# Shared first weight tiles, 512-column values and a wide first norm in a two-layer hybrid decoder

## The chip, the core and the metric

The kernel runs on one core of one Trainium2 chip. A core has engines that each work through their own list of instructions in order: TensorE (PE, matrix products), VectorE (DVE), ScalarE (ACT), GpSimd (POOL) and SyncE (SP, which here only starts transfers). They meet at semaphores. The metric is the time of one execution on the device in microseconds (us), lower is better.

## What is computed

The input is x, 512 positions of 1024 channels in float32. Each of two layers does this:

```python
h = rmsnorm(x, norm1_w[l])
proj = h @ w_in[l]
lx, lg, rq, rk, rv, rg, hq, hf, hi, hg = jnp.split(proj, split_idx, axis=-1)
y_lru = rglru_group(lx, lg, ...)                  # 512 channels
y_ret = retention_group(rq, rk, rv, rg, ...)      # 4 heads of 64
y_hg = hgrn2_group(hq, hf, hi, hg, lb_all[l], ...)  # 4 heads of 64
x = x + jnp.concatenate([y_lru, y_ret, y_hg], axis=-1) @ w_out[l]
h = rmsnorm(x, norm2_w[l])
x = x + conv_ffn(h, ffn_w_up[l], ..., ffn_w_down[l])
```

and a last rmsnorm follows. `rmsnorm` divides by the root of the mean square over the channels and multiplies by a weight. In the HGRN2 group the forget gate is f = lb + (1 − lb)·sigmoid(hf), the key is (1 − lb)·sigmoid(−hf), and the values are the columns `hi`, called hv below; the retention group has queries rq, keys rk and values rv. In both groups a state gathers key times value, so a factor of each position can sit on either. The outputs of both groups are normed by head and gated by rg and hg.

## The kernel before

**Tiles.** x lies as eight tiles x0 to x7 of 128 channels by 512 positions. Full float32 accuracy is had from three products in a rounded format: each operand is split in a high part (xh, wh, written by ACT) and the rest (xl, wl, written by DVE), and `mm3` (line 320) issues high·high, high·rest and rest·high, lines 321 to 323. A product of one weight tile (1024 channels by 128 columns, as 128x1024) is 8 times 3 matmuls into one PSUM bank of 128x512, `pps`. The norm's division by position is left out of the operands and multiplied in when DVE copies the bank out (`ev`, with `rb`, which holds 1/root for every position in 128 equal rows).

**What sets the order.** A planner (`Flow`, `Timed`) runs when the kernel is built: the work is written as chains (generators) that are advanced by estimated costs of operations, and the order in which they ask is the fixed order of every engine's list. `next_w` keeps two weight tiles split ahead of the one in use; transfers go through SP. Waits on banks go through `Slots`: four banks for the products (`mm`), four for small ones (`sm`).

**The first norm** (`finish_norm`, line 419). The squares of x0 to x7 are added into `ssq` (in layer 0 by DVE, in layer 1 by POOL). Four fp32 matmuls give the mean square of each position as a column (`rms_ps`, 128x4), DVE makes the root's reciprocal in 12 tiny operations (`rsqrt_cols`), four more matmuls spread it over the rows (`rms_rps`), ACT copies that to `rb`. The columns (`rms_rc`) also scale the values when ACT copies them out. The second norm of a layer goes another way (`rsqrt_wide`, line 358): two matmuls of 512 columns against ones, then Ln, Exp and Square on ACT and two DVE operations.

**Order of the input products.** hf0 hq0 hf1 hq1 (the f and q of HGRN2, two tiles of 128 columns each), hv, rq0 rk0 rv rq1 rk1, lx0 to lx3, hg0 hg1 rg0 rg1 lg0 to lg3, then the output product `ops`. Tiles go in pairs; in layer 0 the first pair is run part by part as its weights land. `hv` and `rv` are each computed with positions on the rows, in 256 columns: `vps`, 2 layers by 192 matmuls. While the last input products run, DVE has what follows the mixers to do: the norms of the head outputs (`hc_v` to `hc_x`), their gating (`rt_on`, `hg_on`), the recurrence of the RG-LRU (`qp`, `lr_g`), and the split of the results (`xl<-hg_on` first) on which `ops` waits.

**Small set-ups.** `setup_lb` (line 480) makes lb and 1 − lb (`sm_m`, `sm_e`, `lbc`), `setup_small` (line 449) the constants of the RG-LRU (`sp_*`, `lamc`).

Of the kernel before, what the change touches and what calls it, by code (L numbers as in the profile page):

```python
# [15 lines left out]
S = 512  # L16
# [12 lines left out]


FIRST = ["x0", 0, "x1", 1, "x2", "x3", 2, "x4", "x5", 3, "x6", "x7"]
# [17 lines left out]
for _n, _w in (  # L49
# [9 lines left out]
WCOL = {"lx": 0, "lg": 512, "hg": 2816, "rg": 1792}  # L59
TAIL = "lx0 lx1 lx2 lx3 hg0 hg1 rg0 rg1 lg0 lg1 lg2 lg3".split()  # L60
TAIL = [(t[:2], int(t[2])) for t in TAIL]

WIN = (
    [("f", 2304), ("f", 2048), ("f", 2432), ("f", 2176), ("v", 2560, 0), ("v", 2560, 1)]
    + [("f", 1024), ("f", 1280), ("v", 1536, 0), ("v", 1536, 1), ("f", 1152), ("f", 1408)]
    + [("f", WCOL[n] + 128 * j) for n, j in TAIL]
)
WNAMES = (
    [("hf", 0), ("hq", 0), ("hf", 1), ("hq", 1), "hv", None]
    + [("rq", 0), ("rk", 0), "rv", None, ("rq", 1), ("rk", 1)]  # L70
    + TAIL
)
# [136 lines left out]
def kernel(ctx, tc, x_in, win, wout, wup, wdn, lruw, params, consts, out):  # L209
# [26 lines left out]
    lbc = const.tile([128, DEPTH, 2, 2], F32, name="lbc")  # L236
# [25 lines left out]
    for l in range(DEPTH):  # L262
        wlist += [win[l, i] for i in range(len(WIN))]
# [94 lines left out]
    def rsqrt_wide(sq, r, tile_of, weights, name):  # L358
# [11 lines left out]
        A.activation(out=r, in_=ps, func=AF.Ln, bias=eps)  # L370
        yield None
        A.activation(out=r, in_=r, func=AF.Exp, scale=-0.5)
        yield None
        t = sq
        A.activation(out=t, in_=r, func=AF.Square)
        yield None
# [8 lines left out]
    def new_norm(nw, pool):  # L385
        n = Norm()
        n.pool = pool
        n.nw, n.h, n.lo, n.sq, n.rb = nw, {}, {}, 0, None
        n.ssq = None
        n.fast = n.wide = False  # L390
        return n
# [27 lines left out]
    def finish_norm(n):  # L419
        if n.wide:  # L420

            v = rpool.tile([128, S], F32, name="rb")
            yield from rsqrt_wide(n.ssq, v, lambda t, i: rpool.tile([128, S], t, name="sq", bufs=3), ones, "rms_ps")
            n.rb = v
            return
# [3 lines left out]
        yield None  # L429
        rc = rsqrt_cols(rpool, ps, [128, NC], "rms")  # L430
        drop(sm)
        yield None
        n.rc = rc
        ps = yield from psum([128, S], "rms_rps")
        for c in range(NC):
            small(0.22, out=ps[:, c * 128:(c + 1) * 128], lhsT=rc[:, c:c + 1].to_broadcast([128, 128]), rhs=ident)
        yield None
        rb = rpool.tile([128, S], F32, name="rb")
        A.activation(out=rb, in_=ps, func=AF.Copy)
        drop(sm)  # L440
        yield None
        n.rb = rb
# [6 lines left out]
    def setup_small():  # L449
        tp = rpool  # L450
        for l in range(DEPTH):
            lam = pc(l, "lam", 0, 4)
            ab = tp.tile([128, 4], F32, name="sp_ab")
            V.tensor_scalar(out=ab, in0=lam, scalar1=-1.0, scalar2=None, op0=ALU.mult)
            rl = tp.tile([128, 4], F32, name="sp_rl")
            V.tensor_scalar(out=rl, in0=ab, scalar1=0.0, scalar2=None, op0=ALU.max)
            V.tensor_tensor(out=ab, in0=ab, in1=lam, op=ALU.max)
            e = tp.tile([128, 4], F32, name="sp_e")
            A.activation(out=e, in_=ab, func=AF.Exp, scale=-1.0)
            yield None  # L460
            z = tp.tile([128, 4], F32, name="sp_z")
            V.tensor_scalar(out=z, in0=e, scalar1=2.0, scalar2=None, op0=ALU.add)
            V.reciprocal(out=z, in_=z)
            V.tensor_tensor(out=z, in0=z, in1=e, op=ALU.mult)
            z2 = tp.tile([128, 4], F32, name="sp_z2")
            V.tensor_tensor(out=z2, in0=z, in1=z, op=ALU.mult)
            yield None
            s = tp.tile([128, 4], F32, name="sp_s")
            V.tensor_scalar(out=s, in0=z2, scalar1=1.0 / 17.0, scalar2=1.0 / 15.0, op0=ALU.mult, op1=ALU.add)
            for d in (13, 11, 9, 7, 5, 3, 1):  # L470
                V.tensor_tensor(out=s, in0=s, in1=z2, op=ALU.mult)
                V.tensor_scalar(out=s, in0=s, scalar1=1.0 / d, scalar2=None, op0=ALU.add)
                yield None
            V.tensor_tensor(out=s, in0=s, in1=z, op=ALU.mult)
            V.scalar_tensor_tensor(out=s, in0=s, scalar=2.0, in1=rl, op0=ALU.mult, op1=ALU.add)
            for i, f in enumerate((-8.0, -16.0, 8.0)):
                V.tensor_scalar(out=lamc[:, l, :, i], in0=s, scalar1=f, scalar2=None, op0=ALU.mult)
            yield None

    def setup_lb():  # L480
# [18 lines left out]
    def matmul_tiles(n, count, done, first=False, freed=None, joint=False):  # L499


        i = 0
        while i < count:
# [7 lines left out]
            if pair == 1:  # L511
                order = [(0, k) for k in range(KD)]
            else:
                cut = KD - 2
                order = [(p, k) for ks in (range(cut), range(cut, KD)) for p in range(2) for k in ks]
                if joint:
                    order = [(p, k) for k in range(KD) for p in range(2)]
            for p, k in order:
                (wh, wl), ps = got[p]
                if k not in n.lo:  # L520
                    yield lambda: k in n.lo
                o = k * 128
                if joint and pair == 2:
                    wh, wl = got[k // 4][0]
                    o = k % 4 // 2 * 512 + p * 256 + k % 2 * 128
                sl = slice(o, o + 128)
                mm3(ps, wh[:, sl], wl[:, sl], n.h[k], n.lo[k], k == 0, k == KD - 1)
                if freed and i == count - 1:
                    freed(k)
                yield None  # L530
                if k == KD - 1:
                    done(i + p, ps)
# [3 lines left out]
    def mixers(l, n):  # L536
# [8 lines left out]

        def evac(key):
            yield lambda: key in ps_of and n.rb is not None
            yield from ev.take()
            t = mp.tile([128, S], F32, name="ev", bufs=NEV)
            V.tensor_tensor(out=t, in0=ps_of.pop(key), in1=n.rb, op=ALU.mult)  # L550
# [4 lines left out]
        def evac_v(key):  # L555
            yield lambda: key in ps_of and n.rb is not None
# [946 lines left out]
```

## Time and profile before

| | |
|---|---|
| median of 3 runs | 1168.36 us (1167.86 to 1168.49) |
| the profiled execution | 1168.12 us |
| its span, first to last instruction | 1166.3 us |
| granted TensorE clock, mean | 0.998 |
| PE busy | 1154.9 us, 99% |
| DVE busy | 781.1 us, 67% |
| ACT busy | 534.3 us, 46% |
| POOL busy | 64.9 us, 6% |
| chain of work that ended last | PE 96%, DVE 2%, DMA 1% |

The span is the time from the first to the last recorded instruction, 1.82 us short of the execution. Busy time of PE counts overlapping matmuls by their modelled ends; how fast PE really issues is read from the starts of matmuls in the timeline. The chain is followed back from the last instruction to what released each step.

### The profile page before, as it was taken

To read this page: it belongs to the slowest core of one execution; us is meant where nothing else is said; L and a number is where in the kernel's file an instruction comes from. 1 tells how busy PE (TensorE), PEld (TensorE's weight loads), DVE (VectorE), ACT (ScalarE), POOL (GpSimd) and SP (SyncE) were. 2 spreads that over 40 slices of the span, in tenths; PEclk is the share of its full clock that TensorE was granted. 3 is DMA by queue.
4 is the path that set the end of the run, shared out by engine and by line. 5 is a ranking of instruction groups with operands and counts; after the bars stand their busy time and mean duration, and the time that the engine had idled before them with its cause. 6 is when DMAs were issued, how large, how long until landed. Compare 5 with 4: busy or idle time off the path is not lost.

```text
span 1166.3 us, 15226 instructions
## 1 busy us (share of the span) xinstructions
PE 1154.9 (99%) x6046; PEld 961.6 (82%) x6046; DVE 781.1 (67%) x1162; ACT 534.3 (46%) x722; POOL 64.9 (6%) x51
## 2 busy tenths in 40 slices
PE   9999999999999999999999999999999999999997
PEld 7888778888888888888888877888888888888886
DVE  7887887577774575474668486955876646745645
ACT  6536874464443343232542568545444424433422
POOL 1011210000000000000310012100000000000001
PEclk9999999999999999999999999999999999999999
DMA  7232223223323332322432221423232232233222
GB/s 257 94 99 56 72 73 125 92 90 106 93 76 105 109 87 89 113 86 76 126 103 81 73 82 37 140 88 98 91 99 96 80 121 93 76 105 104 82 71 88
DMA packets 36455, 111.79 MB, mean 96 GB/s; under 512 B 4512, under 2 KB 5024, under 8 KB 36384
## 3 DMA queue, kind: packets, MB, share of 16 engines
q1 hardware_dynamic: 34560, 108.59, 29.6%
q10 hardware_dynamic: 1824, 2.23, 0.7%
q8 instruction: 47, 0.77, 0.3%
q14 instruction: 24, 0.20, 0.0%
HBM read 106.61 MB, written 2.10 MB: 93 GB/s over the span
## 4 chain that ended last, share of the span: by engine, by line
PE 96%; DVE 2%; DMA 1%; issue 0%; SPq 0%; ACT 0%; POOLq 0%; POOL 0%; DVEq 0%
PE pps L321 20%; PE pps L323 19%; PE pps L322 19%; PE dps L322 7%; PE dps L321 7%; PE dps L323 7%; PE ops L322 3%; PE ops L321 2%; PE ops L323 2%; PE vps L321 1%; PE vps L322 1%; PE vps L323 1%; PE k_o L327 1%; PE hg_pl L327 1%; PE lr_ps L327 1%; DVE qp L185 1%
## 5 line engine op out<-in xcount | busy, mean ns | idle before, releaser
L321 PE MATMUL pps<-xh,wh 128*128 128x512 f32 x1024 | 403.5, 394 | 0.0
L323 PE MATMUL pps<-xh,wl 128*128 128x512 f32 x1024 | 399.4, 390 | 1.3 <-DVE wl L185 1.3
L322 PE MATMUL pps<-xl,wh 128*128 128x512 f32 x1024 | 398.9, 390 | 0.0
L185 ACT ACTIVATE wh<-raw 128x1024 fp32r<-128x1024 f32 (+3 forms) x211 | 204.8, 973 | 150.5 <-PE dps L322 103.3
L185 DVE TENSOR_TENSOR wl<-raw,wh 128x1024 fp32r<-128x1024 f32 (+3 forms) x211 | 243.2, 1155 | 12.8 <-ACT wh L185 12.8
L321 PEld LDWEIGHTS pps<-xh,wh 128*128 128x128 f32 x1024 | 192.5, 188 | 43.2 <-issue 3.5
L323 PEld LDWEIGHTS pps<-xh,wl 128*128 128x128 f32 x1024 | 192.3, 188 | 42.5 <-DVE wl L185 2.1
L322 PEld LDWEIGHTS pps<-xl,wh 128*128 128x128 f32 x1024 | 192.6, 188 | 39.0 <-DVE xl L185 0.4
L185 DVE SCALAR_TENSOR_TENSOR hs<-pps,rb 128x512 f32<-128x512 f32 x88 | 60.4, 690 | 129.6 <-PE pps L323 129.6
L321 PE MATMUL dps<-gh,wh 128*128 128x512 f32 x320 | 124.5, 389 | 0.0
L322 PE MATMUL dps<-gl,wh 128*128 128x512 f32 x320 | 124.5, 389 | 0.0
L323 PE MATMUL dps<-gh,wl 128*128 128x512 f32 x320 | 124.5, 389 | 0.0
L185 DVE TENSOR_TENSOR x<-x,dps 128x512 f32<-128x512 f32 (+1 forms) x72 | 44.9, 627 | 107.4 <-PE dps L323 107.0
L185 ACT ACTIVATE cg<-hs,prm 128x512 f32<-128x512 f32 x44 | 35.9, 816 | 85.1 <-DVE hs L185 85.1
L185 ACT ACTIVATE cg<-cg 128x512 f32<-128x512 f32 x44 | 27.8, 632 | 93.9 <-DVE cg L185 93.9
L321 PEld LDWEIGHTS dps<-gh,wh 128*128 128x128 f32 x320 | 60.1, 188 | 12.6
L323 PEld LDWEIGHTS dps<-gh,wl 128*128 128x128 f32 x320 | 60.1, 188 | 12.4
L322 PEld LDWEIGHTS dps<-gl,wh 128*128 128x128 f32 x320 | 60.1, 188 | 12.4
L185 DVE SCALAR_TENSOR_TENSOR cvv<-hs,prm,cvv 128x511 f32<-128x511 f32 x88 | 65.9, 748 | 1.8
L185 DVE SCALAR_TENSOR_TENSOR cg<-hs,prm,cg 128x511 f32<-128x511 f32 x88 | 65.7, 747 | 1.5
L185 ACT ACTIVATE gh<-cvv 128x512 fp32r<-128x512 f32 x44 | 27.8, 631 | 73.6 <-DVE cvv L185 73.6
L322 PE MATMUL ops<-xl,wh 128*128 128x512 f32 x128 | 50.1, 391 | 0.0
(218 smaller groups left out, 1275.1 us busy)
## 6 DMA issues: line engine op xcount, KB each, us to landing
raw<-in_wup_dram SPq DMA_DIRECT2D x88, 512.0 KB, 3.5
raw<-in_win_dram SPq DMA_DIRECT2D x46, 512.0 KB, 3.5
raw<-in_wdn_dram SPq DMA_DIRECT2D x48, 384.0 KB, 3.0
raw<-in_wout_dram SPq DMA_DIRECT2D x16, 512.0 KB, 3.5
raw<-in_wdn_dram SPq DMA_DIRECT2D x16, 256.0 KB, 2.6
x<-in_x_dram SPq DMA_DIRECT2D x8, 256.0 KB, 5.3
sw<-ev ACTq DMA_DIRECT2D x32, 64.0 KB, 2.1
raw<-in_win_dram SPq DMA_DIRECT2D x4, 256.0 KB, 5.0
```

Of the source, the lines that this page charges most:

```text
L185: return fn(*args, **kw)
L321: T.matmul(out=ps, lhsT=ah, rhs=bh, start=start, stop=False)
L322: T.matmul(out=ps, lhsT=ah, rhs=bl, start=False, stop=False)
L323: T.matmul(out=ps, lhsT=al, rhs=bh, start=False, stop=stop)
L327: T.matmul(**kw)
```

## The change

**The first four tiles.** hf0, hf1, hq0 and hq1 become one block of 512 columns, stored by parts: a weight tile q holds channels tiles k = 2q and 2q + 1 of all four. `joint_tiles` runs them in both layers, all four products for k = 0 to 5 and then k = 6, 7 of each. In layer 0 x and the parts are loaded in turn, x0, part 0, x1, part 1 and so on.

**Values.** hv and rv, 512 columns together, follow at once: one bank for each 128 positions, matmuls of 512 columns. Two of the four banks are small ones (`sm`). ACT copies them out without a scale.

**First norm.** It is made by `rsqrt_wide` in both layers, with a root on ACT and a reciprocal of 128x512 on DVE in place of Ln and Exp. In layer 1 the squares are added by DVE too (`n.fast`). Its scale, no longer on the values, goes on the keys: on k of HGRN2 in the DVE operation that scales it anyhow, and on rk by evacuating it with rb squared, which ACT makes once per layer.

**Set-ups.** `setup_lb` now stands before the end of the first norm; `setup_small` does both layers at once, mostly on POOL. The ones are made by memset.

```diff
-FIRST = ["x0", 0, "x1", 1, "x2", "x3", 2, "x4", "x5", 3, "x6", "x7"]
+JOINT = [("hf", 0), ("hf", 1), ("hq", 0), ("hq", 1)]
+ALONE = "rq0 rk0 rq1 rk1 lx0 lx1 lx2 lx3 hg0 hg1 rg0 rg1 lg0 lg1 lg2 lg3".split()
...
 def rsqrt_wide(...)
+        if root:
+            A.activation(out=t, in_=ps, func=AF.Sqrt, bias=eps)
+            yield None
+            V.reciprocal(out=r, in_=t)
+            V.tensor_tensor(out=t, in0=r, in1=r, op=ALU.mult)
...
 def finish_norm(n):
-        ps = yield from psum([128, NC], "rms_ps")
-        for c in range(NC):
-            small(0.21, out=ps[:, c:c + 1], lhsT=n.ssq[:, c * 128:(c + 1) * 128], rhs=dmean)
...
-        rc = rsqrt_cols(rpool, ps, [128, NC], "rms")
...
-            small(0.22, out=ps[:, c * 128:(c + 1) * 128], lhsT=rc[:, c:c + 1].to_broadcast([128, 128]), rhs=ident)
...
+        yield from rsqrt_wide(n.ssq, v, lambda t, i: rpool.tile([128, S], t, name="sq", bufs=3), ones, "rms_ps", n.root)
...
+    def joint_tiles(n, done):
+        ws, pss = [], []
+        order = [(k, p) for k in range(KD - 2) for p in range(4)] + [(k, p) for p in range(4) for k in (KD - 2, KD - 1)]
+        for k, p in order:
...
+            mm3(pss[p], wh[:, o:o + 128], wl[:, o:o + 128], n.h[k], n.lo[k], k == 0, k == KD - 1)
...
 def evac(key):
-            V.tensor_tensor(out=t, in0=ps_of.pop(key), in1=n.rb, op=ALU.mult)
+                A.activation(out=rb2[0], in_=n.rb, func=AF.Square, scale=0.5)
...
+            if key[0] == "rk":
+                V.tensor_tensor(out=t, in0=ps_of.pop(key), in1=rb2[0], op=ALU.mult)
+            else:
+                V.scalar_tensor_tensor(out=t, in0=ps_of.pop(key), scalar=-0.5, in1=n.rb, op0=ALU.mult, op1=ALU.mult)
...
 def hg_forget(ft):
-            V.tensor_scalar(out=kt, in0=kt, scalar1=olb, scalar2=None, op0=ALU.mult)
+            V.scalar_tensor_tensor(out=kt, in0=kt, scalar=lbc[:, l, ft, 2:3], in1=n.rb, op0=ALU.mult, op1=ALU.mult)
...
 def mixers(l, n):
-                        for k in range(4):
-                            sl = slice(k * 256, (k + 1) * 256)
...
+                for k in (2 * q, 2 * q + 1):
+                    sl = slice(k % 2 * 512, k % 2 * 512 + 512)
+                    mm3(banks[c], n.h[k][:, ts], n.lo[k][:, ts], wh[:, sl], wl[:, sl], k == 0, k == KD - 1)
...
 def main():
+            tile_w(6)
+            tile_w(7)
+            fetch()
+            setup_lb()
```

How DVE's list changes at two places follows; the names are those of the tiles above, and "x7" behind a row is a count.

The first place is DVE around the first norm of layer 0. Before, from the last split of the start to the norm's tiny operations:

```order
L185 TENSOR_TENSOR wl<-raw,wh 128x1024
L185 TENSOR_TENSOR ssq<-ssq,sq 128x512 x7
L185 TENSOR_TENSOR wl<-raw,wh 128x1024 x2
L185 TENSOR_SCALAR rms_v<-rms_ps 128x4
L185 TENSOR_SCALAR rms_rc<-rms_v 128x4
```

After, a piece that begins within the set-up of lb, whose first row (`sm_m<-prm`) follows right on the seventh addition to `ssq` and on the two halves of the split of part 6 and 7:

```order
L175 TENSOR_TENSOR lbc<-sm_e 128x2
L175 TENSOR_SCALAR lbc<-lbc 128x2 x2
L175 TENSOR_TENSOR wl<-raw,wh 128x1024
L175 TENSOR_TENSOR sq<-ssq,sq 128x512
L175 TENSOR_TENSOR wl<-raw,wh 128x1024
L175 RECIPROCAL rb<-ssq 128x512
L175 TENSOR_TENSOR ssq<-rb 128x512
L175 SCALAR_TENSOR_TENSOR ssq<-rms_ps,ssq 128x512
L175 SCALAR_TENSOR_TENSOR rb<-ssq,rb 128x512
L175 SCALAR_TENSOR_TENSOR ev<-pps,rb 128x512 x4
```

The set-up of lb, 14 tiny operations now, and a weight split stand between the additions and `sq<-ssq,sq`, which is the rest of the split sum: the second of the norm's two matmuls reads it. Before, that set-up stood behind the norm's operations.

The second place is DVE in layer 0 while the last gate products run. The copies out of the two rg tiles stand a few rows above each piece, with the four `qp<-qp,lr_g` operations behind them. Before, from the last of the four:

```order
L185 SCALAR_TENSOR_TENSOR qp<-qp,lr_g_1504 128x512
L185 TENSOR_TENSOR wl<-raw,wh 128x1024 x2
L185 TENSOR_TENSOR ev<-pps,rb 128x512
L185 SCALAR_TENSOR_TENSOR rt_on<-rt_on,prm,ev 128x512 x2
L185 TENSOR_TENSOR qp<-qp,lr_g_1288 128x512
```

After, from the end of the second head norm of retention:

```order
L175 SCALAR_TENSOR_TENSOR hc_nt<-hc_nt,hc_v 128x8
L175 SCALAR_TENSOR_TENSOR hc_x<-hc_nt,hc_rc 128x512
L175 SCALAR_TENSOR_TENSOR ev<-pps,rb 128x512
L175 TENSOR_TENSOR wl<-raw,wh 128x1024
L175 SCALAR_TENSOR_TENSOR rt_on<-rt_on,prm,ev 128x512
L175 TENSOR_TENSOR rt_on<-rt_on,hn_rps 128x512
L175 SCALAR_TENSOR_TENSOR rt_on<-rt_on,prm,ev 128x512
L175 TENSOR_TENSOR qp<-qp,lr_g_1121 128x512
```

That head norm (`hc_v` to `hc_x`, 12 operations) and the operation that applies it (`rt_on<-rt_on,hn_rps`) stood ahead of the copies out of rg before, and stand behind them and behind the four `qp` rows now.

## Rows read from the trace of the kernel before

**Rows 1.** Waits of PE: engine, line, releaser, us in total, times, longest.

```profile
PE pps L323 <- DVE wl L185: 1.3, 2, 0.6
```

**Rows 2.** Timeline, PE, values: start us, us, operation, shapes, count, [idle before].

```profile
38.06 0.28 PE L322 MATMUL vps<-wl,xh 128*128 128x256 f32 x1
...
39.98 0.28 PE L323 MATMUL vps<-wh,xl 128*128 128x256 f32 x1
```

**Rows 3.** Timeline, PE, from the start to behind layer 0's first norm.

```profile
5.25 0.79 PE L321 MATMUL pps<-xh,wh 128*128 128x512 f32 x1
...
7.15 0.39 PE L322 MATMUL pps<-xl,wh 128*128 128x512 f32 x1
...
20.37 0.39 PE L323 MATMUL pps<-xh,wl 128*128 128x512 f32 x1
21.33 1.05 PE L327 MATMUL rms_ps<-csm,ssq 128*128 128x1 f32 x8 [0.57 <-DVE ssq L185]
22.25 0.48 PE L321 MATMUL pps<-xh,wh 128*128 128x512 f32 x1
...
25.52 0.39 PE L323 MATMUL pps<-xh,wl 128*128 128x512 f32 x1
25.86 1.16 PE L327 MATMUL rms_rps<-csm,rms_rc 128*128 128x128 f32 x8
26.77 0.48 PE L321 MATMUL pps<-xh,wh 128*128 128x512 f32 x1
```

**Rows 4.** Timeline, PE, first norm of layer 1, first of its two blocks.

```profile
590.03 0.95 PE L327 MATMUL rms_ps<-csm,ssq 128*128 128x1 f32 x8
590.84 0.48 PE L321 MATMUL pps<-xh,wh 128*128 128x512 f32 x1
```

**Rows 5.** Timeline, PE, second norm of layer 0, by wide products.

```profile
231.86 0.63 PE L327 MATMUL rms_ps<-sq,ones 128*128 128x512 f32 x2
232.32 0.39 PE L321 MATMUL pps<-xh,wh 128*128 128x512 f32 x1
```

**Rows 6.** Timeline, DVE, start and first norm of layer 0.

```profile
4.93 0.75 DVE L185 SCALAR_TENSOR_TENSOR xl<-x,prm,xh 128x512 fp32r<-128x512 f32 x1 [3.91 <-ACT xh L185]
...
10.48 1.41 DVE L185 SCALAR_TENSOR_TENSOR xl<-x,prm,xh 128x512 fp32r<-128x512 f32 x2
11.81 0.68 DVE L185 TENSOR_TENSOR wl<-raw,wh 128x512 fp32r<-128x512 f32 x1
...
15.81 5.47 DVE L185 TENSOR_TENSOR ssq<-ssq,sq 128x512 f32<-128x512 f32 x7
...
25.72 1.22 DVE L185 TENSOR_TENSOR wl<-raw,wh 128x1024 fp32r<-128x1024 f32 x1
26.86 0.15 DVE L185 TENSOR_TENSOR sm_m<-prm 128x2 f32<-128x2 f32 x1
...
28.94 1.28 DVE L185 TENSOR_TENSOR ev<-pps,rb 128x512 f32<-128x512 f32 x2
```

**Rows 7.** Groups by form, DVE: the two forms of RECIPROCAL, xcount | busy us, mean ns.

```profile
L185 DVE RECIPROCAL sp_z<-sp_z 128x4 f32<-128x4 f32 x2 | 0.4, 178 | 0.1
L185 DVE RECIPROCAL fn_r<-fn_t 128x2 f32<-128x2 f32 x2 | 0.3, 166 | 3.3 <-ACT fn_t L185 3.3
```

**Rows 8.** Timeline, DVE, the end of layer 0's mixers and of layer 1's.

```profile
140.53 1.75 DVE L185 SCALAR_TENSOR_TENSOR hc_x<-hc_nt,hc_rc 128x512 f32<-128x512 f32 x1
...
154.39 0.69 DVE L185 TENSOR_TENSOR ev<-pps,rb 128x512 f32<-128x512 f32 x1 [4.45 <-PE pps L323]
...
176.50 1.28 DVE L185 TENSOR_TENSOR xl<-hg_on,xh 128x512 fp32r<-128x512 f32 x2
...
747.33 1.28 DVE L185 TENSOR_TENSOR xl<-hg_on,xh 128x512 fp32r<-128x512 f32 x2
```

**Rows 9.** Timeline, PE, the first matmul of the output product in each layer.

```profile
176.89 0.39 PE L321 MATMUL ops<-xh,wh 128*128 128x512 f32 x1
...
750.27 0.39 PE L321 MATMUL ops<-xh,wh 128*128 128x512 f32 x1
```

**Rows 10.** Timeline, DVE, beside POOL's additions at the start of layer 1.

```profile
581.64 4.14 DVE L185 TENSOR_TENSOR wl<-raw,wh 128x1024 fp32r<-128x1024 f32 x2
```

More of the change, by code (lines that the diff above doesn't have):

```diff
@@ L389, in new_norm @@
         n.ssq = None
-        n.fast = n.wide = False
+        n.fast = False
+        n.root = True
         return n
@@ L449, in setup_small @@
     def setup_small():
[L450 to L459, printed above, removed]
-            yield None
[L461 to L478, printed above, removed]
@@ L510, in matmul_tiles @@
                 got.append((w, ps))
[L511 to L532, printed above, removed]
+            cut = KD - 2 if pair == 2 else KD
+            for ks in (range(cut), range(cut, KD)):
+                for p in range(pair):
+                    (wh, wl), ps = got[p]
+                    for k in ks:
+                        if k not in n.lo:
+                            yield lambda: k in n.lo
+                        sl = slice(k * 128, (k + 1) * 128)
+                        mm3(ps, wh[:, sl], wl[:, sl], n.h[k], n.lo[k], k == 0, k == KD - 1)
+                        if freed and i == count - 1:
+                            freed(k)
+                        yield None
+                        if k == KD - 1:
+                            done(i + p, ps)
             i += pair
@@ new lines, in done @@
+        def done(i, ps):
+            ps_of[JOINT[i]] = ps
+        yield from joint_tiles(n, done)
+        banks = []
+        for q in range(4):
+            wh, wl = yield from next_w()
+            for c in range(NC):
+                ts = slice(c * 128, (c + 1) * 128)
+                if q == 0:
+                    sl, pool, tag = ((sm, sm_ps, "sm") if c < 2 else (mm, mm_ps, "mm"))
+                    yield from sl.take()
+                    banks.append(pool.tile([128, 512], F32, name="vps", tag=tag))
+                for k in (2 * q, 2 * q + 1):
+                    sl = slice(k % 2 * 512, k % 2 * 512 + 512)
+                    mm3(banks[c], n.h[k][:, ts], n.lo[k][:, ts], wh[:, sl], wl[:, sl], k == 0, k == KD - 1)
+                    yield None
+                if q == 3:
+                    ps_of["v", c] = banks[c]
@@ new lines, in begin @@
+            for k in range(6):
+                tile_x(k)
+                tile_w(k)
+                if k == 1:
+                    raws[3] = rawp.tile([128, 1024], F32, name="raw")
+                    piece(6)
+                    piece(7)
+                    nc.sync.dma_start(out=csm, in_=consts[:, 0:CSMALL])
+                    fl.load(128 * 4 * CSMALL)
+                    nc.sync.dma_start(out=prm[:, 8:], in_=params[:, 8:])
+                    fl.load(128 * 4 * (DEPTH * PL))
+                if k in (3, 5):
+                    fetch()
+                if k > 1:
+                    square(k - 2)
@@ L1360, in begin @@
+            for k in (6, 7):
+                tile_x(k)
+                square(k - 2)
+            square(6)
+            last = square_x(n, 7)
+            next(last)
+            next(last)
+            tile_w(6)
+            tile_w(7)
+            fetch()
+            setup_lb()
+            fl.free.update(A=17.8, V=19.0)
+            fl.now = 5.2
+            fl.spawn(last, 11.5)
             yield 15.5
```

287 lines of the change are left out of this document (127 added, 160 removed).

## Prediction

> **What bounds the kernel now.** The view to read first is the chain of work that ended last, as the table above gives it: 96% of it is PE. The waits of PE come next, since they say what PE stands still for. The largest entry is 1.3 us, two stalls on a weight split [rows 1]. So PE's own list sets the time, and an edit is worth what it takes out of or puts into the spacing of PE's matmuls, plus any new wait. For the spacing I read the timeline of PE, by the starts of matmuls and not by their durations, because they overlap: from 7.15 to 20.37 us 58 products of 512 columns start 0.228 us apart [rows 3]; 16 values of 256 columns take 39.98 − 38.06 = 1.92 us, 0.120 each [rows 2]. Last I read DVE's timeline at the two places where the change alters its list, because DVE, with 67% busy, is the engine that can come too late there.
>
> **Values.** 384 matmuls of 256 columns become 192 of 512. 384 × 0.120 = 46.1 us go and 192 × 0.228 = 43.8 us come: −2.3 us. All of it is on the path, since PE is. That half the count buys so little is plain from the rows: a matmul of 256 columns already costs barely over half of one of 512. The bounds are −2.6 and −2.0, by 0.001 us on either spacing.
>
> **Norm on PE.** In layer 0 the old norm breaks PE's row twice. From the last product before it (20.37) to the first behind (22.25) there are 1.88 us where 0.23 would do, so the first block costs 1.65, a wait of 0.57 for DVE among it. The second costs 26.77 − 25.52 − 0.23 = 1.02 [rows 3]. In layer 1 each of the two blocks has the price of the one shown, 590.84 − 590.03 = 0.81 [rows 4]. Together 4.3 us go. The two wide matmuls that come take 232.32 − 231.86 = 0.46 in each layer, as the second norm shows [rows 5]: +0.9. Sum −3.4.
>
> **The wait that comes with it.** The second wide matmul reads the rest of the split sum, and DVE makes that rest behind a longer row of work. I count from DVE's first operation at 4.93 [rows 6]. Eight `xl`: two of them take 11.81 − 10.48 = 1.33, so 5.3. Eight half splits at 0.68 less the 0.07 by which neighbours overlap: 4.9. Seven additions that wait for one another: 5.5. That is 20.6. The set-up of lb, now in front, has 14 tiny operations; twelve took 28.94 − 26.86 = 2.08, so 2.4. One split of 1024 takes 26.86 − 25.72 = 1.14, and the rest itself 0.68. That makes 24.9, and about 0.4 more for waits on ACT and on landings early on, as DVE's row of before has them: 25.3. PE has 72 products ahead of the norm; before, the 63rd stood at 20.37, so the 72nd stands at 20.37 + 9 × 0.228 = 22.4 and the second wide matmul could start at 22.9 [rows 3]. PE waits 2.4 us (1 to 3: less if the additions hide in DVE's idle time, more if the weights land late). Queued behind it on PE are the last 24 of the joint products, then all else. The old wait of 0.57 is in the term above.
>
> **The reciprocal.** None of 512 elements is in the trace. The two forms there take 166 ns for 2 elements and 178 for 4 [rows 7]. From below, another operation of that size takes 0.68 [rows 6]; by the slope of 6 ns per element it is 0.17 + 510 × 0.006 = 3.2 us; from above, in proportion to 4 elements, 22.8. I take 3.2, because the slope is the only one of the three that uses both rows. What covers it: behind the norm PE has 24 joint products and 12 value products that need no bank from DVE, 36 × 0.228 = 8.2 us. DVE and ACT need about 0.5 for the sum, 0.6 for the root, the reciprocal, then three operations of 0.68 and the first copy out, 0.7: 3.9 and the reciprocal. So it is hidden up to some 4.3 us, and every us beyond costs one in layer 0; layer 1 has the sum ready earlier. Cost 0.
>
> The Trainium skill ("VectorE: DVE Perf Modes", section "First, the fixed hardware budget") says that the reciprocal is an iterative divide with a repeat count of 8. A plain operation costs (0.68 − 0.15) / 510 = 1.04 ns per element by the trace, so by that rule, as an estimate, it is 8.3 ns per element, 4.4 us, and the sum would be 0.1 higher; the rows' slope of 6 lies between.
>
> **Start.** The first product now needs a whole half tile split (0.68) where a quarter did; but PE issues its first four products in 7.15 − 5.25 = 1.90 us, 0.48 each [rows 3], twice as long as later, and a later first product meets less of this stretch. +0.1 (0 to 0.3).
>
> **End of the mixers, layer 0.** Before, DVE was just in time: from the copy of rg1 (154.39) it worked without a gap to the split of hg_on at 176.50, 22.1 us, and PE took up the output product at 176.89 [rows 8, 9]. Now the second head norm of retention lies in this stretch: 11 tiny operations (2.1), hc_x (0.68 if alone, 1.75 as it stood) and one more of 0.68, +3.4 at least: 25.5. PE gets longer too, since the head norm's two blocks of matmuls move with it, about 1.0 each like the blocks of [rows 3], and loses the 0.7 us of its stall: 22.5 − 0.7 + 2.0 = 23.8. DVE is 1.7 late, less the old stall that goes: +1.0, and 0.2 for the splits behind. +1.2 (0 to 3).
>
> **End of the mixers, layer 1.** There the split stood at 747.33 and the product at 750.27, 2.9 us to spare [rows 8, 9], which the same 3.4 uses up, and the other stall of [rows 1] goes. −0.3 (−0.8 to 0.8).
>
> **Start of layer 1.** Four banks must be open at once where two did, so the fourth product waits for the last addition to x; DVE no longer runs beside POOL's additions, where two splits took 4.14 us instead of 2.3 [rows 6, 10]. Both land within 0.1 of each other: +0.1 (0 to 0.5).
>
> The Trainium skill ("SBUF — State Buffer", section "Who interferes with whom") says that a DVE operation with two SBUF inputs contends with a POOL one that reads SBUF. The 4.14 us agree [rows 10]; by that rule the squares' move to DVE frees layer 1's start, and the set-ups moved to POOL stretch DVE by a few tenths at most.
>
> **At nothing.** The scale on the keys changes operations that were there; the square for rk, one ACT operation per layer, lies where ACT is half idle; `setup_small` on POOL is needed only by the RG-LRU. If that cover were gone, it would be under 1 us.
>
> **Sum.** −2.3 − 3.4 + 2.4 + 0.1 + 0 + 1.2 − 0.3 + 0.1 = −2.2 against the profiled 1168.12, which lies 0.24 below the median: 1165.9 us.
>
> **Rivals.**
> A: neither new wait arises. If DVE's additions run into its idle time and the planner's order leaves the head norm room, +2.4 and +1.2 go: 1162.3. For it: DVE's first operation had waited 3.91 us and others at the start waited too, so that seven additions can go in between [rows 6]. Against it: even without the additions' 5.5 us DVE's list comes to 19.8, and they do not vanish, they only fill gaps. 20%.
> B: the clock. If PE, standing 2.4 us, falls to the lower of its two levels and starts again as at the beginning, where products took 0.48 instead of 0.23, it loses between 1.0 (four products, [rows 3]) and 3.6 (half of the 7.15 us): 1167 to 1169.5. Against it: behind the 0.57 us of waiting in layer 0 the next products came at full rate. 7%.
> C, the slower side: the end of the mixers on DVE. POOL's products run in the same stretch, and what they stretch is 1.14 to 2.07 for a split [rows 6, 10] and 0.68 to 1.75 for hc_x [rows 8]. With four such operations more beside POOL, some 4.2 us, layer 0 loses 4.2 and layer 1, its room used up, 1.3: 1171.4. It decides once the split of hg_on in layer 0 starts over 30 us behind rg1's copy. 10%.
> D: the reciprocal is proportional, 22.8 us: 18 exposed in layer 0, some 15 in layer 1, about 1199. 2%.
> E, that the change doesn't do what it says: the values of 512 columns keep PE as long as the 384 did, because a bank or a split is late between them: +2.3, 1168.2. 4%.
>
> **How the numbers follow.** The forecast, both waits about as sized, has 57%, with its own range 1164.0 to 1167.8. A measurement of this kernel tells about 0.2% from no change, which is below 1166.0 or above 1170.7. Half of the forecast's share lies below 1166.0, and all of A: 49% faster. C and D make 12% slower. The rest, 39%, is the same. For the range, 1162.0 to 1169.0 leaves out C, D and the far parts of A and B, about two in ten.
>
> **What would show it.** Values 0.228 apart, 192 of them; one block of two `rms_ps` per layer; a wait of PE for the second of them in layer 0 of 1 to 3 us on DVE; a RECIPROCAL of 3 to 4.4 us with no PE wait between the norm and the values; the two stalls on a weight split gone and `ops` in layer 0 waiting for `xl<-hg_on` about 1.7 us. A granted clock below its level behind the norm, an `ops` wait over 4 us or a reciprocal above 5 us would make it wrong.

## The result, and the profile after

The changed kernel takes 1177.22 us, median of 4 (1176.50 to 1177.53), against 1168.42 for the kernel before on the same chip (1167.86 to 1168.53): a ratio of 1.0072, 95% interval 1.006 to 1.0084. It is 0.72% or 8.8 us slower; the forecast was 2.2 us faster. The profiled execution took 1176.99 us, with a span of 1175.2 and a mean granted clock of 0.993 (before 0.998).

The page of the kernel after, busy time and the chain that ended last:

```profile
PE 1157.6 (99%) x5826; PEld 949.5 (81%) x5826; DVE 784.8 (67%) x1110; ACT 535.3 (46%) x719; POOL 56.9 (5%) x67
...
PE 92%; DVE 6%; issue 1%; DMA 1%; ACT 0%; SPq 0%; POOL 0%; POOLq 0%; DVEq 0%
```

PE is still 99% busy, which says nothing, as overlapping matmuls hide pauses. The chain says more: 6% of it is DVE's now, where it was 2%. The waits of PE, which answer to [rows 1]:

```profile
PE ops L312 <- DVE xl L175: 2.7, 1, 2.7
PE rms_ps L317 <- DVE sq L175: 1.4, 1, 1.4
PE rms_ps L317 <- ACT sq L175: 1.4, 1, 1.4
...
PE pps L313 <- DVE wl L175: 0.6, 1, 0.6
```

Three waits of over 1 us are new, and of the two stalls on a weight split one is left. A smaller new one, not shown here, is 0.72 us in layer 0 at 126.32, where the matmuls that spread the first head norm (`hn_rps`) wait for DVE. Where the time went is read from the starts of PE's first and last matmuls of each stretch. The column "forecast" sorts the terms of the sum into the same stretches.

| stretch | before | after | difference | forecast |
|---|---|---|---|---|
| first product to first `ops`, layer 0 | 171.6 | 174.4 | +2.8 | −1.6 |
| output product, layer 0 | 43.9 | 48.2 | +4.4 | +1.9 |
| FFN, layer 0 | 359.5 | 359.6 | +0.1 | 0 |
| input products, layer 1 | 170.0 | 169.4 | −0.6 | −2.5 |
| output product and FFN, layer 1 | 405.1 | 406.1 | +1.1 | 0 |
| last product to the end | 11.0 | 12.0 | +1.1 | 0 |
| sum, with 0.1 ahead of the first product | | | +8.9 | −2.2 |

In the row of layer 1's output product and FFN the two parts go opposite ways: the output product took 1.6 more (43.29 to 44.93), the FFN 0.6 less (361.77 to 361.21).

The first norm of layer 0 on PE's timeline (start us, us, operation, shapes, count, idle before), to be read against [rows 3]:

```profile
22.16 0.39 PE L313 MATMUL pps<-xh,wl 128*128 128x512 f32 x1
23.95 0.50 PE L317 MATMUL rms_ps<-sq,ones 128*128 128x512 f32 x1 [1.40 <-ACT sq L175]
25.87 0.79 PE L317 MATMUL rms_ps<-sq,ones 128*128 128x512 f32 x1 [1.42 <-DVE sq L175]
26.46 0.63 PE L311 MATMUL pps<-xh,wh 128*128 128x512 f32 x1
26.89 0.63 PE L312 MATMUL pps<-xl,wh 128*128 128x512 f32 x1
...
28.60 0.63 PE L313 MATMUL pps<-xh,wl 128*128 128x512 f32 x1
29.02 0.49 PE L311 MATMUL pps<-xh,wh 128*128 128x512 f32 x1
```

Each of the two wide matmuls waits 1.4 us, one for ACT and one for DVE. Behind them six products stand 0.43 apart, where 0.23 is the rule: PE runs at its lower clock. The same happens at the start of layer 0's output product, which answers to [rows 9]:

```profile
179.79 0.40 PE L311 MATMUL ops<-xh,wh 128*128 128x512 f32 x1
182.85 0.80 PE L312 MATMUL ops<-xl,wh 128*128 128x512 f32 x1 [2.66 <-DVE xl L175]
183.44 0.63 PE L313 MATMUL ops<-xh,wl 128*128 128x512 f32 x1
183.87 0.63 PE L311 MATMUL ops<-xh,wh 128*128 128x512 f32 x1
...
185.58 0.63 PE L312 MATMUL ops<-xl,wh 128*128 128x512 f32 x1
186.00 0.50 PE L313 MATMUL ops<-xh,wl 128*128 128x512 f32 x1
186.34 0.39 PE L311 MATMUL ops<-xh,wh 128*128 128x512 f32 x1
```

By stretches (us from and to, length, busy us and count of PE, PEld, DVE, ACT, POOL, then PE's granted clock, DMA share, GB/s) the clock there is 0.50, which is 1.2 of 2.4 GHz:

```profile
178.00:182.80 4.80, 2.19 (x10) 1.47 (x8) 4.80 (x7) 2.84 (x5) 0.00 (x0) 1.00 0.23 91
182.85:186.20 3.35, 3.35 (x8) 2.70 (x9) 3.35 (x6) 1.13 (x2) 0.00 (x0) 0.50 0.54 157
186.30:200.00 13.70, 13.70 (x61) 11.22 (x61) 8.71 (x12) 5.79 (x9) 0.00 (x0) 1.00 0.33 111
```

DVE over the same end of the mixers, which answers to [rows 8]: the copy of rg1, the retention head norm that has moved behind it, and the split for which `ops` waits.

```profile
156.21 0.69 DVE L175 SCALAR_TENSOR_TENSOR ev<-pps,rb 128x512 f32<-128x512 f32 x1 [4.80 <-PE pps L313]
...
162.56 0.15 DVE L175 TENSOR_SCALAR hc_v<-hn_ps 128x8 f32<-128x8 f32 x1
...
164.76 0.69 DVE L175 SCALAR_TENSOR_TENSOR hc_x<-hc_nt,hc_rc 128x512 f32<-128x512 f32 x1
...
182.12 1.28 DVE L175 TENSOR_TENSOR xl<-hg_on,xh 128x512 fp32r<-128x512 f32 x2
```

The values, against [rows 2], the first and the last of 39 matmuls in a row:

```profile
33.25 0.39 PE L311 MATMUL vps<-wh,xh 128*128 128x512 f32 x1
...
42.12 0.40 PE L313 MATMUL vps<-wh,xl 128*128 128x512 f32 x1
```

(42.12 − 33.25) / 38 = 0.2334 us apart, not 0.228. A difference of 5 ns looks like nothing, but some 4,500 gaps behind matmuls of 512 columns are in this trace. Layer 1's output product has the same spacing, here in the kernel after:

```profile
779.78 0.40 PE L311 MATMUL ops<-xh,wh 128*128 128x512 f32 x1
...
783.28 0.40 PE L311 MATMUL ops<-xh,wh 128*128 128x512 f32 x1
```

15 steps in 3.50 us, 0.2333 each. The kernel before takes 0.2267 at this place. I summed what lies above 0.2267 over all gaps between 0.215 and 0.242 that follow a 512-column matmul, and call it the excess of the spacing: 1.7 us before, 5.6 after, nearly all of it in the mixers and the output products and none in the FFN.

### The profile page after: what moved, and what is told of

It is laid out like the page before. It is cut to its first block, busy times and chain, and to the rows that moved or that the text cites. A ratio compares the mean times of both kernels' runs of the same rounds, so it can differ in the third digit from the quotient of the medians.

```text
span 1175.2 us, 14760 instructions
## 1 busy us (share of the span) xinstructions
PE 1157.6 (99%) x5826; PEld 949.5 (81%) x5826; DVE 784.8 (67%) x1110; ACT 535.3 (46%) x719; POOL 56.9 (5%) x67
## 4 chain that ended last, share of the span: by engine, by line
PE 92%; DVE 6%; issue 1%; DMA 1%; ACT 0%; SPq 0%; POOL 0%; POOLq 0%; DVEq 0%
PE pps L311 18%; PE pps L313 18%; PE pps L312 18%; PE dps L311 7%; PE dps L313 7%; PE dps L312 7%; PE ops L312 3%; PE ops L313 3%; PE ops L311 2%; PE vps L311 1%; DVE qp L175 1%; PE k_o L317 1%; PE hg_pl L317 1%; PE vps L313 1%; PE vps L312 1%
## 5 line engine op out<-in xcount | busy, mean ns | idle before, releaser
L175 ACT ACTIVATE wh<-raw 128x1024 fp32r<-128x1024 f32 (+2 forms) x212 | 204.8, 968 | 144.1 <-PE dps L312 103.3
L175 DVE TENSOR_TENSOR wl<-raw,wh 128x1024 fp32r<-128x1024 f32 (+2 forms) x212 | 238.6, 1128 | 15.9 <-ACT wh L175 15.9
```

Of the source, the lines that this page charges most:

```text
L175: return fn(*args, **kw)
```

## The experiments

Two causes stood out, the waits (with the clock behind them) and the spacing. The spacing changed in stretches whose instructions the change does not touch, so I looked at where the tiles lie. `lbc` has a third column now, and with it the pool of xh and xl starts 32 bytes later. Between that pool and the weights three small tiles of the old norm are gone and one (`mean`) has come, so that wh and wl start 32 bytes earlier than before. Before, every operand starts at a multiple of 128 bytes. After, xh and xl stand 32 past one and the weights 96; in the FFN both operands stand at 96.

**Old places.** Two unused tiles put the pools back.

```diff
-    const.tile([128, 32], F32, name="pad")
-    rpool.tile([128, 32], F32, name="pad")
+    const.tile([128, 24], F32, name="pad")
+    rpool.tile([128, 48], F32, name="pad")
```

> The changed kernel with its two empty pad tiles resized so that the operand tiles (xh, xl, wh, wl) start where they do in the kernel before: the added third column of lbc had moved them by 32 bytes. In the changed kernel matmuls of 512 columns stand 229 to 233 ns apart in the mixers and the output product and 227 in the FFN; before, 227 nearly everywhere. Summed over the matmuls that is 5.6 us above 227 against 1.7 before. Theory 1 (the addresses set the pitch): the pitch returns to 227, the sum to under 2 us, the time to 1173 to 1174 us. Rival (the pitch follows from what interrupts the row of matmuls, not from addresses): pitch and time stay, 1177 us.

1174.44 us (ratio to before 1.0049, 1.0032 to 1.0066), 2.8 less than the changed kernel. The excess of the spacing falls from 5.6 to 2.3 us. The output product of layer 1:

```profile
779.76 0.39 PE L312 MATMUL ops<-xl,wh 128*128 128x512 f32 x1
...
783.16 0.39 PE L312 MATMUL ops<-xl,wh 128*128 128x512 f32 x1
```

15 steps in 3.40 us, 0.2267. So the places cost about a third of the loss; the lists of all engines are those of the changed kernel.

**New places in the kernel before.** The same two tiles there, with 40 and 16.

> The kernel before with its two pad tiles resized so that the operand tiles start where they do in the changed kernel, 32 bytes off; nothing else. Theory 1 (addresses set the pitch): matmuls of the mixers 229 ns or more apart, the time 2 to 4 us up, 1170 to 1172 us. Rival: unchanged, 1168.4 us.

1169.25 us against 1168.37 (ratio 1.0007, 0.9997 to 1.0016). The excess rises from 1.7 to 3.6 us; the time by 0.9, less than expected and within what can be told from no change. The trace shows why: products of 256 columns, which the excess leaves out, come closer together in the new places. The 384 values with the gaps behind them take 46.52 us for 47.99, and the FFN of layer 1, which ends in 192 such products, 361.20 for 361.77. So in this kernel the new places give back what they take. Sixteen steps of the values, 1.88 us for the 1.92 of [rows 2]:

```profile
37.23 0.28 PE L322 MATMUL vps<-wl,xh 128*128 128x256 f32 x1
...
39.11 0.28 PE L323 MATMUL vps<-wh,xl 128*128 128x256 f32 x1
```

**All operands shifted alike.** In the kernel before, only the first of the two tiles is larger (40 for 32), so that activations and weights all stand at 32 past a multiple of 128.

> The kernel before with all operand tiles moved by the same 32 bytes, where e2 moved xh and xl up by 32 and wh, wl and everything behind them down by 32. If the absolute place decides (a boundary of 64 bytes): pitch in the mixers 229 ns, as in e2. If the distance between the two operands of a matmul decides: pitch 227 ns, as before.

One execution, 1168.95 us; the excess is 1.7, as in the kernel before, and the values take 47.98 us, as there. So as far as these places go, the place as such changes nothing; the distance between the two operands does. Only two distances were measured, none and 64 bytes within 128, and why the distance matters is not shown by any run here.

**The rest of the norm's sum first.** For the two waits at the norm I took DVE's row as the cause: the set-up of lb and a split stand ahead of `sq<-ssq,sq`.

```diff
             tile_w(7)
+            next(last)
+            next(last)
             fetch()
             setup_lb()
```

> The changed kernel; in layer 0 the rounded copy and the rest of the split sum of squares (ACT sq<-ssq, DVE sq<-ssq,sq) stand right behind the additions, ahead of the set-up of lb and of the next weight split; nothing else moved by hand. In the changed kernel PE waits 1.4 us twice there and then runs 6 matmuls at the lower clock. Theory 2 (the place of these two operations in the lists makes the wait, and the wait makes the clock fall): both waits go, the granted clock behind the norm stays at its upper level, -4 to -4.5 us: 1172.5 to 1173.5. Rival (it is given back: the reciprocal's chain behind it then holds the first copies and PE waits for a bank): -2 us or less, with a wait of 1 to 2 us at vps.

1174.95 us (1.0064, 1.0043 to 1.0085), 2.3 less, but not as expected. The planner moved the norm's matmuls from behind 72 products to behind 51, and PE waited there all the same. Its profiled execution, which at 1179.81 us is the longest of its four, shows:

```profile
PE rms_ps L317 <- ACT sq L175: 3.6, 1, 3.6
PE pps L313 <- DVE wl L175: 2.7, 2, 2.1
```

The wait of `ops` is gone there, because PE is later. The run tells nothing about the cause; it shows that an order planned from estimates moves elsewhere when one row is moved.

**The same, with the matmuls held** behind 72 products (`fl.spawn(last, 16.3)` for 11.5):

> The changed kernel; as in e3 the rounded copy and the rest of the sum of squares stand ahead of the set-up of lb and of the weight splits in layer 0, but the two norm matmuls stay in their place behind 72 products, which e3 had let slip forward. Theory 2 (their place in the lists of ACT and DVE makes the wait, and the wait makes the clock fall): both waits of 1.4 us go and the clock stays up; -4 to -4.5 us, 1172.7 to 1173.2. Rival (given back): the set-up of lb and two weight splits now stand between the rest and the reciprocal, the copies out come no earlier, and PE waits 1.5 to 2.5 us at the third block of values instead; -2 us or less.

1174.40 us (1.0051, 1.0036 to 1.0066), 2.8 less. Both norm waits and the low clock behind them are gone. But a wait for a bank has come in the middle of the values:

```profile
31.53 0.39 PE L313 MATMUL vps<-wh,xl 128*128 128x512 f32 x1
33.86 0.50 PE L311 MATMUL vps<-wh,xh 128*128 128x512 f32 x1 [1.94 <-DVE ev L175]
```

The bank is freed by the first copy out (`ev`), which needs the reciprocal. In the changed kernel PE came to this place later, by its two waits, and met no wait.

**The products of the recurrence earlier.** DVE stands idle for 4.80 us ahead of rg1's copy. So I let the four `qp` be asked for together with ACT's part, ahead of the copies.

```diff
                 av[j] = a
-            yield None
-            for j in js:
                 V.scalar_tensor_tensor(out=xcs[j], ...)
```

> The changed kernel; the four DVE operations qp<-qp,lr_g of the RG-LRU are issued right behind the ACT operations of their tile, so that they fall into the 4.8 us in which DVE stands idle ahead of the copy of rg1. In the changed kernel PE waits 2.7 us in the output product of layer 0 for xl<-hg_on and then runs 7 matmuls at the lower clock. Theory 3 (DVE's list behind rg1 is what is late): the wait goes, the clock stays, -4 to -4.5 us: 1172.5 to 1173.5. Rival (not DVE's load but the chain of the head norm itself sets it): the wait stays above 1.5 us, -1 us or less.

1182.50 us (1.0119, 1.0104 to 1.0135), 5.3 more.

```profile
PE ops L312 <- DVE xl L175: 6.9, 4, 2.7
```

`hc_v` stayed at 162.55 us, so the head norm is what is late, and filling DVE's idle time with other work does not bring it forward. The order of the lists has put it there. Its matmuls (`hn_ps`) stand on PE at 158.8 us in the changed kernel and at 161.6 in this one, and they need a square which stands on ACT behind all of the recurrence. ACT in the changed kernel, the first and the last of twelve operations of the recurrence, and the square that the head norm needs:

```profile
146.30 0.72 ACT L175 ACTIVATE lr_a<-lr_g,lamc 128x512 f32<-128x512 f32 x1
...
153.62 0.72 ACT L175 ACTIVATE lr_g<-lr_g,lamc 128x512 f32<-128x512 f32 x1
154.25 0.62 ACT L175 ACTIVATE sq<-rt_on 128x512 f32<-128x512 f32 x1
```

**The head norm ahead of them.** One step in the chain lets the planner put `sq<-rt_on` behind the first three of the twelve.

```diff
                 av[j] = a
+                if j == 0:
+                    yield None
```

> The changed kernel; in both layers ACT's twelve operations of the RG-LRU (lr_a, qp, lr_g from lr_g) are parted behind the first three, so that the square for the second head norm of retention (sq<-rt_on) need not stand behind all of them, 8 us long in the trace; its matmuls and DVE's hc_v to hc_x then come ahead of the copy of rg1, where DVE stood idle for 4.8 us. Theory 3 (DVE's list behind rg1 is what is late, and the wait makes the clock fall): the 2.7 us wait for xl<-hg_on in layer 0 shrinks below 0.5, no fall of the clock there, -3.5 to -4.5 us: 1172.7 to 1173.7. Rival (other DVE work moves in and the list stays as long, as in e4): the wait stays above 1.5 us, less than -1 us.

1170.74 us (1.002, 1.001 to 1.003), 6.5 less. DVE in this kernel:

```profile
155.13 0.17 DVE L175 TENSOR_SCALAR hc_v<-hn_ps 128x8 f32<-128x8 f32 x1 [1.02 <-PE hn_ps L317]
...
158.68 0.69 DVE L175 SCALAR_TENSOR_TENSOR ev<-pps,rb 128x512 f32<-128x512 f32 x1 [0.64 <-PE pps L313]
...
180.34 1.29 DVE L175 TENSOR_TENSOR xl<-hg_on,xh 128x512 fp32r<-128x512 f32 x2
```

The head norm stands ahead of rg1's copy again, as in the kernel before. From that copy to the split are 21.7 us (25.9 in the changed kernel, 22.1 before). `ops` begins at 181.36 and no longer waits, the clock stays up, and layer 0's output product takes 43.7 us. The ten executions lie far apart, from 1168.46 us with a mean granted clock of 0.997 to 1173.43 with 0.993: the norm waits are still there, and the mean clock differs from one execution to the next. The profiled one (1172.90, 0.993) has twelve products at the lower clock, all behind the norm, where the changed kernel's has six; where the clock fell in the others is not recorded. Of the 6.5 us between the medians the two traces show 4.5 in layer 0's output product and 0.6 in the input products of layer 1, where the stall on a weight split is gone.

**Three edits together**: old places, head norm early, and the start rearranged with the set-up of lb split in two.

> The changed kernel with the three repairs at once: old tile addresses (e1), the head norm early (e5), and a start in which the rest of the squares comes first (e6), the set-up of lb parted so that its tiny operations stand partly ahead of the last additions and partly behind the first copies out. If the three causes are what cost the time and add up: -2.8, -4 and -4 from 1177.2, so 1166 to 1167, 0.1 to 0.2% below the kernel before, with PE waiting under 1 us in all ahead of the last norm. Rival (what is gained at one place is lost at the next, since DVE's list decides anyway): 1169 or more.

1173.44 us (1.0039, 1.0024 to 1.0054). The start was mended, `ops` was reached at 174.42, and there PE waited:

```profile
PE ops L312 <- DVE xl L175: 5.3, 2, 4.9
```

The planner, with other times at the start, had put DVE's work at the end of the mixers in another order. The gain was lost at the next place.

**Places and head norm.** The next kernel was meant to combine the first and the fifth edit, but it also lacks the two steps that put the last square of x and its addition ahead of the last splits, so they came later.

> The changed kernel with two of the edits tried before: the tiles of the operands start where they did in the kernel before (the first run, -2.8 us), and the first four instructions of the layer-0 head norm are let go one step earlier (the fifth run, -6.5 us). Theory: the two causes lie in different places and add, so 1177.2 - 2.8 - 6.5 = 1167.9 us, 0.5 under the kernel before; matmul pitch excess near 2.4 us, no wait of the layer-0 output product on xl, the two norm waits near 1.4 to 2.4 us each left as they were. Rival: the planner's order comes out otherwise with both edits, or a gain is given back at the next place, as it was when three edits were put together (1173.4): 1170 or more.

1169.75 us (1.0011, 1.0002 to 1.0021). The norm's waits are down to 0.3 and 0.2 us, as its matmuls now stand behind 84 products; but the first of them begins 1.2 us later than with the head norm edit alone (25.56 for 24.36), a split and two small casts have come ahead of the first copy out of a bank (35.38 for 33.48), and the values wait 3.9 us for it. It does not answer the question it was made for. The kernel that does has exactly the two edits, and the lists of all engines are those of the fifth (the 3 us named in what was expected of it are 1.2, as just said):

> The two edits of the run on addresses and of the run on the head norm, and nothing else; every engine's list is that of the latter word for word, only the tiles' places differ. (The earlier run meant to be this one also took two steps out of the start: the last square of x and its addition were left to the planner, its norm came 3 us later, and so it says nothing on whether the two causes add.) Theory: they add, 1170.7 - 2.8 = 1167.9 us, pitch excess 2.2 to 2.4 us, both norm waits as they were. Rival: what the places save is given back as longer waits for the first norm, since DVE and ACT do not get faster with PE: about 1 us less in the start, 1169 to 1170.

1167.01 us against 1168.64 (0.9987, 0.9978 to 0.9996). That is 10.2 less than the changed kernel and 3.7 less than with the head norm alone. Some of the 3.7 is the clock: the executions with a mean of 0.997, four of the one kernel and six of the other, are on average 2.6 apart. So the places are worth 2.6 to 3.7, and the first experiment's 2.8 lies in it. The two causes add as far as this can tell, and more than the whole loss is explained. The spacing's excess is 2.15 us, there is no wait of `ops`, and the norm's two waits remain:

```profile
24.42 0.51 PE L317 MATMUL rms_ps<-sq,ones 128*128 128x512 f32 x1 [1.90 <-ACT sq L175]
26.34 0.50 PE L317 MATMUL rms_ps<-sq,ones 128*128 128x512 f32 x1 [1.42 <-DVE sq L175]
```

**With the start held as well** (the sixth edit), and once more with the set-up of lb 8 us of the plan later:

> The former edits and a third: the rest of the first norm stands ahead of the setup of layer 0's decay on VectorE and its matmuls are held behind 72 products (the sixth run, -2.8 us). Theory of three separate causes: 1177.2 - 2.8 - 6.5 - 2.8 = 1165.1 us, below the kernel before (1168.4) by 3; no norm wait, no clock fall before 170 us, first product of the layer-0 output product near 177.7, none of its matmuls over 0.3 us apart; a wait of 1 to 2 us of the values' matmuls on the first eviction on VectorE stays. Rival: what the start gains is lost at the end of the mixers, since PE reaches the output product 2 us earlier and its first operand is then late again: a wait of 1 to 3 us on xl with low clock behind it, 1168 or more.

> As the run before, but the setup of layer 0's decay is put 8 us of the plan later instead of right behind the rest of the norm, so that the first eviction of the values does not queue behind it. Theory: the values' wait of 1 to 2 us goes as well, 1163.5 to 1165 us. Rival: the setup, now later, pushes VectorE's list at the end of layer 0's mixers back by its own length, about 3 us, and the output product waits on xl for what the start gains: 1166 to 1169.

The first takes 1166.74 us (0.9986, 0.9978 to 0.9995), 0.3 less than without the third edit, which is no difference that can be told. Its first `ops` stands at 176.15, 3.2 earlier than in the profiled execution of the former kernel (that one, 1168.61, is among the longer of its eleven, this one, 1165.85, the shortest), and a wait for a bank takes the place of the norm's waits:

```profile
PE vps L311 <- DVE ev L175: 1.8, 1, 1.8
```

The second takes 1169.02 us (1.0007, 0.9998 to 1.0016): that wait is down to 0.4, `ops` begins at 174.05 and then waits 4.7 us on `xl` in two waits. That is what its rival had, for one of two reasons: at the second wait DVE is late (the fifth split begins at 181.46 for 177.78 in the kernel just before), but at the first the split is not (175.58 for 175.37), and it is PE that comes 2.1 earlier.

## Why the prediction was wrong

Two steps failed. The first is the waits, the clock behind them put at nothing: the norm on PE with its wait was to take 2.9 us in layer 0 and took 5.3, and the output product of layer 0 was to lose 1.9 and lost 4.4. The second is the spacing of the matmuls, which I carried over from the kernel before and to which I gave no term for the places of the tiles; they cost 2.8 us. The parts follow.

**Values, −2.3.** The count is right, the spacing was not. All `vps` matmuls with the gaps behind them take 47.99 us before and 46.30 after, −1.7. With the operands in their old places they take 45.43 (the two-edit kernel), −2.6. I took 0.228 from [rows 3] for granted, for an operand whose place in the SBUF the change moves, and the 0.120 of [rows 2] belongs to the old places as well. In the new ones the values of 256 columns take 46.52 (the second experiment). So half the count is worth 2.6 us in the old places and 0.2 in the new.

**The norm on PE and its wait, −3.4 and +2.4.** Two wide matmuls per layer came, as said. In layer 0 they were to take 0.46 and a wait of 2.4, 2.9 in all. From 22.16 to 26.46 it is 4.30 − 0.23 = 4.1, and six products at the lower clock add 6 × 0.20 = 1.2. DVE's row to the second matmul's operand was nearly right, 25.81 at its end for 25.3:

```profile
25.13 0.68 DVE L175 TENSOR_TENSOR sq<-ssq,sq 128x512 fp32r<-128x512 f32 x1
```

PE was there 0.3 earlier than forecast, and behind the second matmul, which already runs at the lower clock, the next follows after 0.59 instead of 0.23. With the 0.5 on DVE that makes the 1.2 between 2.9 and 4.1. What I did not see is that the first operand comes from ACT, which is held up by the same set-up of lb:

```profile
22.23 0.20 ACT L175 ACTIVATE sm_e<-sm_e 128x4 f32<-128x4 f32 x1 [2.71 <-DVE sm_e L175]
22.34 1.04 ACT L175 ACTIVATE wh<-raw 128x1024 fp32r<-128x1024 f32 x1
23.28 0.61 ACT L175 ACTIVATE sq<-ssq 128x512 fp32r<-128x512 f32 x1
```

ACT waits 2.71 us for one tiny operation in the middle of that set-up, and a split stands ahead of the square too. So PE stood twice. That added no waiting, since the first matmul, begun at 23.95, was over long before 25.81; whether two waits instead of one matter to the clock is not shown. And rival B, the clock, came true at 7% chance: I had argued from the one wait of 0.57 us of [rows 3], which says nothing of five times as much.

**The reciprocal, hidden.** Right: neither `rb` nor a copy out of a bank made PE wait in the changed kernel, and the size from the two rows' slope, 3.2, was close:

```profile
27.42 3.35 DVE L175 RECIPROCAL rb<-ssq 128x512 f32<-128x512 f32 x1 [0.47 <-ACT ssq L175]
```

The estimate of 4.4 from the repeat count of 8 in the Trainium skill ("VectorE: DVE Perf Modes", section "First, the fixed hardware budget") was too high; the measurement decides for 6.3 ns per element, (3.35 − 0.15) / 510, instead of 8.3. It is hidden in part behind the norm's own waits: where these were removed and the set-up of lb stood ahead of the reciprocal, the values waited 1.8 to 1.9 us for a bank. With that set-up moved behind the first copies out, the reciprocal began 1.3 earlier (25.41 for 26.69) and that wait was down to 0.4. So it was mostly the set-up's place that PE paid for, not the reciprocal's length.

**End of the mixers, layer 0, +1.2.** The list was right: 25.5 us of DVE from rg1's copy to the split were forecast, 182.12 − 156.21 = 25.9 measured; PE needed 23.6 for 23.8. C's point, 30 us, was not reached, so the operations were not stretched as C needs. What failed is the lateness. The second matmul of `ops` follows 0.23 us on the first and needs the end of the split, 0.68 behind its start: 2.66 of waiting, not 1.7. Behind it the clock fell and took some 1.5 more (0.36 on the late matmul, six gaps of 0.20). So this stretch lost 4.4, and the early head norm gave it back. The moved head norm's price, 3.4 us, was sound; what I had not asked is why it moved, which is its square's place behind twelve operations on ACT.

**Layer 1, −2.5 for its input products.** −0.6 was measured. The excess of the spacing took 1.2 (1.9 for 0.7), and the stall on a split stayed (0.7). PE was also held 0.5 ahead of a `lr_ps`; what made up for that I did not trace. With the places alone put back the stretch takes 168.6 us, −1.4. In the two-edit kernel, where the stall is gone too, it takes 750.05 − 582.42 = 167.6, −2.4: the term was sound for a kernel with the old places and without the stall.

**What had no term.** The output product of layer 1 lost 1.6 us, of which 1.2 is the spacing (1.23 of excess for 0); the FFN behind it won 0.6 back, as its last products are of 256 columns. The last norm lost 1.1; four of its matmuls ran at a lower clock:

```profile
1166.75 1.22 PE L317 MATMUL fn_rps<-csm,fn_r 128*128 128x128 f32 x4 [1.14 <-DVE fn_r L175]
```

Before they took 0.71. The other half lies behind POOL's last operation, where only the transfers of the output are left: 4.5 us for 4.1. In the kernel before with all operands shifted the same end takes 4.7, so this half says nothing of the change.

**The sum.** Against the forecast the changed kernel is 11 us worse. The two-edit kernel takes 10.2 of them away and stands 1.6 us under the kernel before, where the forecast for the changed kernel was 2.2 under it. That the two totals are so near is in part luck. In the profiled execution of the two-edit kernel the first stretch is 2.3 over the kernel before, where −1.6 was forecast, for the norm's waits are still there; the output product of layer 0 is 0.4 under it, where +1.9 was forecast; layer 1's input products came out as forecast. What the forecast had too small is the order at the end of the mixers (6.5 between medians, the low clock behind it included), and what it left out is the places of the tiles (2.6 to 3.7). What the norm's waits cost by themselves is not settled: where they were removed, the next wait took most of it.

## What to carry to other kernels

Before a term is taken from the spacing of matmuls, see whether the change alters the size of any tile, for then the pools behind it move: compare the start of activations and of weights before and after. If their distance changed, the old spacings do not hold; here products of 512 columns got slower by it and those of 256 faster. An operation that moves on one engine is priced by what it waits for on the others (here a square behind twelve operations of ACT), and a wait on PE by the matmuls behind it at the lower clock as well. Edits to an order that a planner makes are tried one at a time and then together, since the planner gives back at the next place what it gained at the last.

## What the runs showed of the hardware that I had not expected

**Matmul spacing and places.** Products of 512 columns follow one another every 0.2267 us where both operands start at the same place within 128 bytes (0, 32 or 96: the kernel before, that with all operands shifted, the FFN of the changed one), and on average every 0.229 to 0.2333 us where one starts at 32 and the other at 96. The first value shows in the input products, the second in the values and in layer 1's output product. Products of 256 columns go the other way: most stand 0.120 us apart at the same place and 0.113 to 0.118 at 32 and 96. Why layer 0's output product lost less (0.4 us of excess for 1.2 in layer 1) is open; with the new places in the kernel before, and in the kernels of the experiments on the rest of the sum and on `qp`, layer 1's lost 0.4 too.

**The clock behind a wait.** After two waits of 1.4 us with one matmul between them six products ran at 1.2 GHz, in other kernels with the same two waits eight to thirteen. After the wait of 2.66 us for `xl` it was six again, while in the kernel with the norm held and in that with the old places a wait of 2.7 at the same place was followed by the full rate (granted clock 1.00 in both). After the 1.77 us among the values the rate stayed full. In the two-edit kernel the mean granted clock of eleven executions runs from 0.994 to 0.997 and the time from 1169.33 to 1165.89 us with it.
